# Four edits to an encoder step: decayed rows read from the accumulator, v's pieces over two steps, later background sums, a row scale from a sum of squares

## The chip, the cores and the metric

The kernel runs on one core of a Trainium2 chip. Its engines are named as the profile names them: PE is TensorE's matrix product and PEld its weight load, DVE is VectorE, ACT is ScalarE, POOL is GpSimd and SP is SyncE, which here only issues transfers. Times are microseconds on the device. The kernel before was run three times: 3076.58, 3070.44 and 3073.78 us; the median is 3073.78. One further execution was profiled, and all rows below come from it.

## What is computed

One layer of a streaming encoder, on 4096 prompt rows and 32 sample rows of width 1024. Every row is normalised, scaled and shifted (by vectors that come from a conditioning vector c), and multiplied by one wide weight w_in. The product is cut into z, x, B, C, dt, u, v and a gate g for two mixers. Both results go side by side through w_out, and the rows are normalised again and added to the input.

```
h = rms_norm(x, g_pre) * (1 + scale) + shift                 # scale, shift from silu(c) @ w_ada + b_ada
z, xbc, dt_raw, u, v, gt = split(h @ w_in)

# mixer A: 16 heads of 64 channels, state 128 long
xbc = silu(causal_conv(xbc))                                 # 4 taps; gives xs, B, C
dt  = softplus(dt_raw + dt_bias);  a = -exp(a_log)
a_cum = cumsum(dt * a)                                       # within a chunk
decay = exp(a_cum[l] - a_cum[s]) for s <= l, else 0
y_diag = ((C . B) * decay * dt) @ xs                         # within the chunk
decay_end = exp(a_cum[last] - a_cum)
chunk_states = B^T @ (decay_end * dt * xs)                   # what the chunk adds to the state
h_c = exp(a_cum[last]) * h_(c-1) + chunk_states              # carried from chunk to chunk
y = y_diag + exp(a_cum) * (C @ h_prev) + d_skip * xs
ssd_out = y * silu(z)

# mixer B: 8 groups of 128 channels, chunks of 128 rows
v_n = layer_norm(v)
gmlp_out = silu(gt) * u * (tril(w_s) @ v_n + b_s)

out = x + gate * rms_norm(concat(ssd_out, gmlp_out) @ w_out)
```

Beside the rows, the last conv inputs, the last state and the sample's v_n are returned.

## The kernel before

**Blocks and steps.** The prompt goes through in NB = 8 blocks of T = 512 rows; the sample's 32 rows ride along in block 3. Channels stand on the partitions, rows in the free direction. A block consists of nine steps k = 0 to 8 over w_in, two column groups of 256 a step (the table `SUPER`): step 0 makes B and C, step 1 the first two pairs of heads p0 and p1 (x and z of 128 channels each), steps 2 to 7 a pair p(k) and a group g(k-2) of mixer B, step 8 the groups g6 and g7. Between step 0 and step 1 lie the output projection of the block before (`out_proj`, drawn through the generator `outs`) and the product for v (`v_stage`). All wide products are made in float16 with each operand split into a high and a low part, three matrix products for one (`PARTS`): the high part is an ACT copy, the low part a subtraction on DVE or POOL (`split`, L274 and L275).

**Two forms of the product.** Blocks 0 and 1 use plain products (`plain_step`, weight tiles of 512 KB, four a step). Blocks 2 to 7 use a seven-product scheme of Strassen's kind (`super_step`, seven tiles a step, products 256 rows wide). It needs sums of weight blocks, which are made once. That is the background work of the first two blocks: in block 0 the weights are loaded, scaled and split (`stage_load`, `stage_scale`), and in block 1 `sums_load`, `sums_scale`, `sums_first` and so on load pairs of them again from DRAM, add and subtract them on DVE, split them on DVE and POOL and store the sums (L395 to L431). A sums job works in one of three areas of SBUF; the list `places` in block 1 gives each job the point at which it starts, and its area.

**What sets the order.** There are two devices. `later(n, f)` puts a function into a list that `tick()` works off: f issues its instructions n ticks later. TensorE's loops call `tick` every twelve products in a `super_step`, 14 ticks a step, and every six in a `plain_step`, 16 ticks a step; an output projection has 64 ticks, v 32. So the lag of a `later` is a place in TensorE's stream of products. Then a scheduler puts each engine's instructions in an order by the priority with which they were issued: `shifted(-150, f)` makes f more urgent, `behind` makes the sums' functions less urgent by 200. Each engine works off its own order strictly, so an instruction that waits holds up all behind it. Loads stand on SP's queue in the same way: weights (wt, wm), the rows L and E, and the sums' loads are behind one another there.

**The path of one pair of heads.** The conv (`conv`, DVE, three to four passes, then a SiLU on ACT, L805) gives xsT. `pair_rows` loads the two rows of cumulative decay as L and E (L1125 loads E), `pair_decay` and `pair_exp` make the decay from them on ACT and `pair_mask` multiplies by C.B on POOL. `pair_xt` (L1152) transposes xsT on TensorE into an accumulator bank ps_xt. `pair_xdt` multiplies it by dt on DVE, from the bank into xdt; `pair_xde` multiplies xdt by the decay to the chunk's end on POOL, into xde (both L1167, in `pair_times`). `pair_state` (L1175) makes the chunk states ps_s from xde on TensorE, `pair_carry` (L1197) carries the state from chunk to chunk on DVE into hc, and `pair_y` makes ps_y from xdt and L and ps_o from hc. `pair_sum`, `pair_gate` and `add_mix` join them. The factors dt, a_cum and the decay to the end (tile dep, array st.de) are made once a block in `dt_cumsum` (L889: a subtraction from an accumulator bank on DVE, L891: exponential on ACT).

**v.** `v_stage` makes v for the four chunks of 128 rows of a block, `v_moments` and `v_norm` their means and scales, and then each chunk's two halves are normalised on DVE into a piece vt of 128x512 (`v_split_half`, L1078) and split (ACT, POOL). Eight pieces a block, for which `v_split` is called at ticks 0, 3, 6 and 9 and its halves one tick apart. A vt lies in one of five buffers (`tmp2(prompt, ...)`), which it shares with E and with other intermediate tiles, mx and ms among them.

**Row scale.** Before the first block, gcol and scol (the scale and shift of a row, for 16 combinations of column tile and stream) are multiplied by a power of two a_sc, so that the float16 parts of h are in range. It comes from the bound max(|gcol| sqrt(1024) + |scol|), over the partitions by a transpose and a product on TensorE (L644 to L665). In the sources as in the profile, ps_... are accumulator banks (eight), hTp the normalised rows, wt and wm weights, xp the x columns of the product with their halo, zs the z columns.

## Time and profile before

| | |
|---|---|
| median of three runs | 3073.78 us |
| the profiled execution, time | 3074.91 us |
| its span | 3073.2 us |
| busy: PE, DVE, ACT, POOL | 2830.3, 1746.7, 1529.6, 1281.7 us |
| mean granted clock of TensorE | 0.972 of full speed |

The span is the time from the first to the last instruction that the profiler saw. TensorE is busy most of it. A row of the view of waits gives the idle time of an engine just ahead of a group of its instructions, by what ended it; for TensorE those are the places in which products stood still. The boundaries of the stretches, read from the timeline: block 0 about 62 to 410 us, the output projection and v of block 1 to 575, block 1's steps to 862, then blocks 2 to 7 of some 320 to 380 us each up to 2966, and the last output projection. A granted clock of 1.00 is 2.4 GHz, 0.50 is 1.2 GHz.

### The profile page before, as it was taken

What the parts mean: (1) busy time and instruction counts of PE and PEld (TensorE: products, weight loads), DVE (VectorE), ACT (ScalarE), POOL (GpSimd) and SP (SyncE); (2) the same over time, 40 slices, a digit from 0 to 9 for tenths busy, and PEclk for the clock granted to TensorE, in tenths of its full rate; (3) what the DMA queues carried; (4) which work ended last, traced back from release to release, by engine and by line L of the source; (5) the groups of instructions that cost most, each with busy time, mean ns of one, the idle gap of its engine ahead of it and who ended that gap; (6) DMA issues with size and microseconds to landing.
All of it is one profiled execution on the core that took longest, in us unless ns stands there. A gap on an engine that the chain in (4) does not pass through costs nothing.

```text
span 3073.2 us, 54218 instructions
## 1 busy us (share of the span) xinstructions
PE 2830.3 (92%) x20754; PEld 1881.3 (61%) x20754; DVE 1746.7 (57%) x3808; ACT 1529.6 (50%) x3234; POOL 1281.7 (42%) x1193
## 2 busy tenths in 40 slices
PE   7989898688999999989998999999999999999987
PEld 2434443344655887458874588747885588648863
DVE  4768686775664556355564554735455544526452
ACT  4577654567653554436544355444544354415531
POOL 2456654576632443224542245323543254204540
PEclk8999999899999999999999999999999999999999
DMA  9766468876435665265562666546663666556652
GB/s 316 237 211 199 146 203 297 267 240 212 151 104 201 200 195 177 90 205 178 179 201 75 215 201 195 176 155 211 192 214 102 222 195 188 182 173 198 197 159 57
DMA packets 269053, 577.36 MB, mean 188 GB/s; under 512 B 27898, under 2 KB 115170, under 8 KB 268792
## 3 DMA queue, kind: packets, MB, share of 16 engines
q1 hardware_dynamic: 246840, 500.86, 51.5%
q0 software_dynamic: 21952, 73.04, 6.4%
q8 instruction: 162, 2.65, 0.4%
q14 instruction: 99, 0.81, 0.1%
HBM read 499.82 MB, written 73.97 MB: 187 GB/s over the span
## 4 chain that ended last, share of the span: by engine, by line
PE 42%; DVE 12%; ACT 8%; DMA 5%; POOL 5%; issue 2%; SPq 0%; POOLq 0%; ACTq 0%; DVEq 0%
PE ps_proj L778 18%; PE ps_out L951 11%; PE ps_v L1016 5%; DMA wm<-vd 2%; DVE ms L1289 2%; DMA L<-acdp 2%; PE ps_y L1208 2%; PE ps_s L1175 1%; DVE vt L1078 1%; PE ps_out L1375 1%; POOL acc L1102 1%; POOL mix L1242 1%; PE ps_o L1212 1%; ACT L805 1%; DMA E<-acdp 1%
## 5 line engine op out<-in xcount | busy, mean ns | idle before, releaser
L778 PE MATMUL ps_proj<-hTp,wt 128*128 128x256 f16 x9072 | 1047.4, 274 | 44.6 <-ACT zs L731 26.5
L778 PEld LDWEIGHTS <-wt 128*128 128x128 f16 x9072 | 887.6, 98 | 157.2 <-issue 41.2
L951 PE MATMUL ps_out<-wm,mix 128*128 128x512 f16 x2880 | 646.2, 382 | 29.3 <-DVE dep L889 15.3
L951 PEld LDWEIGHTS <-mix 128*128 128x128 f16 x2880 | 280.9, 98 | 356.7 <-issue 28.1
L749 PE MATMUL ps_proj<-hTp,wt 128*128 128x512 f16 x1728 | 401.8, 389 | 2.5 <-DMA wt<-wd 2.5
L749 PEld LDWEIGHTS <-wt 128*128 128x128 f16 x1728 | 171.3, 100 | 203.0 <-issue 20.1
L1134 ACT ACTIVATE L<-L,acp 128x128 f32<-128x128 f32 x512 | 166.8, 391 | 165.6 <-DMA L<-acdp 150.5
L1016 PE MATMUL ps_v<-wm,hTp 128*128 128x512 f16 x1008 | 222.6, 381 | 17.8 <-DMA wm<-vd 17.8
L1224 POOL TENSOR_TENSOR mix<-mix,E 128x512 f32<-128x512 f32 x64 | 95.5, 1492 | 308.4 <-DVE E L1220 308.4
L1145 POOL TENSOR_TENSOR L<-L,cb 128x512 f32<-128x512 f32 (+1 forms) x144 | 168.1, 1180 | 104.7 <-ACT L L1139 103.0
L729 DVE SCALAR_TENSOR_TENSOR xp<-ps_proj,scw,xp 128x256 f32<-128x256 f32 x132 | 62.4, 480 | 233.5 <-PE ps_proj L778 221.5
L1016 PEld LDWEIGHTS <-hTp 128*128 128x128 f16 x1008 | 98.7, 98 | 139.2 <-issue 22.1
L818 DVE SCALAR_TENSOR_TENSOR xsT<-xp,cols,xsT 128x512 f32<-128x512 f32 (+1 forms) x216 | 182.8, 849 | 1.7
L275 POOL TENSOR_TENSOR mix<-ms,mix 128x512 f16<-128x512 f32 x64 | 90.8, 1421 | 220.6 <-ACT mix L274 220.6
L1102 POOL TENSOR_TENSOR acc<-acc,sq 128x512 f32<-128x512 f32 (+1 forms) x126 | 148.3, 1178 | 43.9 <-ACT sq L1098 42.4
L275 POOL TENSOR_TENSOR v<-vt,v 128x512 f16<-128x512 f32 (+1 forms) x66 | 83.7, 1297 | 174.9 <-ACT v L274 174.8
L275 POOL TENSOR_TENSOR hTp<-ta,hTp 128x512 f16<-128x512 f32 x60 | 71.3, 1189 | 202.7 <-ACT hTp L274 202.6
L810 ACT ACTIVATE halo_p<-xp 128x3 f32<-128x3 f32 x96 | 19.5, 203 | 220.5 <-DVE xp L729 219.9
L1167 POOL TENSOR_TENSOR xde<-xdt,dep 128x512 f32<-128x512 f32 x64 | 70.8, 1107 | 138.1 <-DVE xdt L1167 129.2
L274 ACT ACTIVATE mix<-ms 128x512 f16<-128x512 f32 x128 | 79.5, 627 | 83.4 <-DVE ms L1289 82.7
L1175 PE MATMUL ps_s<-xde,bt 128*128 128x128 f32 (+1 forms) x528 | 79.5, 296 | 41.2 <-POOL xde L1167 41.2
L1098 ACT ACTIVATE sq<-mix 128x512 f32<-128x512 f32 x120 | 74.8, 626 | 78.4 <-POOL mix L1242 59.0
(428 smaller groups left out, 4703.9 us busy)
## 6 DMA issues: line engine op xcount, KB each, us to landing
wt<-wd SPq DMA_DIRECT2D x414, 512.0 KB, 4.1
wm<-od SPq DMA_DIRECT2D x104, 512.0 KB, 3.5
wm<-vd SPq DMA_DIRECT2D x92, 512.0 KB, 4.9
L<-acdp SPq DMA_DIRECT2D x128, 256.0 KB, 4.1
sums<-in_w_in_dram SPq DMA_DIRECT2D x38, 512.0 KB, 6.5
wd<-wt POOLq DMA_DIRECT2D x36, 512.0 KB, 4.8
stg<-in_w_in_dram SPq DMA_DIRECT2D x64, 256.0 KB, 5.2
E<-acdp SPq DMA_DIRECT2D x128, 128.0 KB, 4.4
```

The costliest lines, as they stand in the source:

```text
L274: nc.scalar.activation(hi, src, AF.Copy)
L275: eng.tensor_tensor(lo, src, hi, op=ALU.subtract)
L749: nc.tensor.matmul(ps[pi].rearrange("p (h t) -> p h t", h=2), wt[:, pi, a, q * P:(q + 1) * P], prompt.h[:, 2 * kh:2 * kh + 2, b, q, :], st ...
L778: nc.tensor.matmul(ps, wt[:, pi, a, q * P:(q + 1) * P], prompt.h[:, slot, b, q, :], start=(starts and h == 0 and n == 0), stop=(n == 11), ...
L818: nc.vector.scalar_tensor_tensor(dst, xp[:, k:k + Ts], w(k), dst, op0=ALU.mult, op1=ALU.add)
L951: nc.tensor.matmul(ps[c], x(kk, a, c), w[:, kk, b, :], start=(first and n == 0), stop=(last and n == 5))
L1016: nc.tensor.matmul(ps, prompt.h[:, slot, a, q, i * P:(i + 1) * P], wt[q // 2][:, q % 2, b, :], start=(starts and n == 0), stop=(n == 11), ...
L1102: eng.tensor_tensor(st.accb if last else st.acc, st.acc, sq, op=ALU.add)
L1134: nc.scalar.activation(L[:, c, :], L[:, c, :], AF.Relu, scale=-1.0, bias=st.ac[:, c, 2 * j + hh:2 * j + hh + 1])
L1145: nc.gpsimd.tensor_tensor(w.L[hh], w.L[hh], st.cb[j // 4][0:st.Q], op=ALU.mult)
L1175: nc.tensor.matmul(ps_s[:, c * P:(c + 1) * P], st.bt[j // 4][0:st.Q, c, :], w.xde[:, c, :], start=True, stop=True)
L1224: nc.gpsimd.tensor_tensor(w.m, w.m, w.E, op=ALU.add)
```

## The change

Four places are changed.

1. `dt_cumsum` multiplies st.de by dt on DVE, behind the exponential. `pair_xdt` then makes both xde and xdt on DVE, each straight from the accumulator bank, xde first; `pair_xde` on POOL is gone.
2. The eight pieces of v come one every four ticks, first halves of the four chunks at ticks 0, 4, 8 and 12, second halves at 16 to 28, over two steps instead of one; the split follows two ticks later instead of one. (`v_split` is gone. The sample's pieces come at ticks 0 and 4.)
3. Sums jobs start at ticks 40 + 16n and 48 + 16n instead of 18 + 18n and 27 + 18n of block 1. The third area's places are as before.
4. The row scale comes from the sum of squares of gcol sqrt(2048) and scol sqrt(2), with two ACT instructions, one product on TensorE (`ssq_total`) and the helper that other scales use (`pow2_of_ssq`).

```diff
-    bnd = const.tile([P, 2, KT], F32, name="bnd")
...
-    nc.vector.tensor_scalar(bnd, gcol, math.sqrt(DM), None, op0=ALU.mult)
...
-    nc.vector.tensor_reduce(bmx, bnd, axis=AX.XY, op=ALU.max)
-    ps = psum("ps_bmx")
-    nc.tensor.transpose(ps[0:1, 0:P], bmx, ident)
...
-    nc.vector.tensor_scalar(a_inv.bitcast(I32), e_i, B23, -12.0 * B23, op0=ALU.mult, op1=ALU.add)
+    sq2 = const.tile([P, 2], F32, name="sq2")
+    sqj = const.tile([P, 2, 2 * KT], F32, name="sqj")
+    for i, (t, f) in enumerate(((gcol, math.sqrt(2 * DM)), (scol, math.sqrt(2.0)))):
+        nc.scalar.activation(sqj[:, i], t.rearrange("p s k -> p (s k)"), AF.Square, scale=f, accum_out=sq2[:, i:i + 1])
+    nc.vector.tensor_tensor(sq2[:, 0:1], sq2[:, 0:1], sq2[:, 1:2], op=ALU.add)
+    pow2_of_ssq(ssq_total(sq2[:, 0:1]), [P, 1], "wp", a_sc, a_inv)
...
         nc.scalar.activation(st.de, st.de, AF.Exp)
+        nc.vector.tensor_tensor(st.de, st.de, st.dt, op=ALU.mult)
+        st.dd = st.de
         later(9, dt_rows, st)
...
         for c in range(n):
-            later(3 * c, v_split, st, c, mv, r)
+            sp = st.v[c].bitcast(F16).rearrange("p (h a d) -> p h a d", h=2, a=2)
+            st.vsplit.append(sp)
+            for half in range(2):
+                later((4 if st is prompt else 1) * (c + 4 * half), v_split_half, st, c, half, sp, mv, r)
...
-    def v_split(st, c, mv, r):
-        Q = st.Q
-        sp = st.v[c].bitcast(F16).rearrange("p (h a d) -> p h a d", h=2, a=2)
-        for half in range(2):
-            later(half, v_split_half, st, c, half, sp, mv, r)
-        st.vsplit.append(sp)
...
-        later(1, split, sp[0:Q, half, 0], sp[0:Q, half, 1], t, nc.gpsimd)
+        later(2, split, sp[0:Q, half, 0], sp[0:Q, half, 1], t, nc.gpsimd)
...
     def pair_xdt(st, j, w, ps):
         Q, n, nm = st.Q, st.nch, st.name
-        w.xdt = wk.tile([P, n, P], F32, tag="xdt" + nm, name="xdt", bufs=1)[0:Q]
-        pair_times(st, j, nc.vector, w.xdt, ps[0:Q, 0:n * P].rearrange("q (c m) -> q c m", c=n), st.dt)
-        later(1, shifted, -150, pair_xde, st, j, w)
-
-    def pair_xde(st, j, w):
-        w.xde = wk.tile([P, st.nch, P], F32, tag="xde" + st.name, name="xde", bufs=1)[0:st.Q]
-        pair_times(st, j, nc.gpsimd, w.xde, w.xdt, st.de)
+        w.xdt, w.xde = [wk.tile([P, n, P], F32, tag=t + nm, name=t, bufs=1)[0:Q] for t in ("xdt", "xde")]
+        src = ps[0:Q, 0:n * P].rearrange("q (c m) -> q c m", c=n)
+        pair_times(st, j, nc.vector, w.xde, src, st.dd)
+        pair_times(st, j, nc.vector, w.xdt, src, st.dt)
...
-            places = [(18 + 18 * n, f[:, 0:3072]) for n in range(10)]
-            places += [(27 + 18 * n, f[:, 3072:6144]) for n in range(9)]
+            places = [(40 + 16 * n, f[:, 0:3072]) for n in range(10)]
+            places += [(48 + 16 * n, f[:, 3072:6144]) for n in range(9)]
             places += [(114 + 30 * n, spare(prompt.h)) for n in range(3)]
```

TensorE's own order is the same in both kernels but for ten places where neighbours change. The order of DVE moves at three kinds of place. The first is DVE behind v of block 4, at about 1754 us of the trace: vt are v's pieces, xp and zs the columns of the product, the last row the conv of pair p0. Before:

```order
L1078 TENSOR_SCALAR vt<-v,mvp,nrp 128x512 x8
L729 SCALAR_TENSOR_TENSOR xp<-ps_proj,scw,xp 128x256 x2
L729 SCALAR_TENSOR_TENSOR zs<-ps_proj,scw,zs 128x256 x2
L729 SCALAR_TENSOR_TENSOR xp<-ps_proj,scw,xp 128x256
L815 TENSOR_SCALAR xsT<-xp,cols 128x512
L818 SCALAR_TENSOR_TENSOR xsT<-xp,cols,xsT 128x512
```

In the changed kernel (its lines are numbered some 13 to 18 lower) the same place reads:

```order
L1063 TENSOR_SCALAR vt<-v,mvp,nrp 128x512 x5
L716 SCALAR_TENSOR_TENSOR xp<-ps_proj,scw,xp 128x256
L1063 TENSOR_SCALAR vt<-v,mvp,nrp 128x512
L716 SCALAR_TENSOR_TENSOR xp<-ps_proj,scw,xp 128x256
L716 SCALAR_TENSOR_TENSOR zs<-ps_proj,scw,zs 128x256 x2
L716 SCALAR_TENSOR_TENSOR xp<-ps_proj,scw,xp 128x256
L802 TENSOR_SCALAR xsT<-xp,cols 128x512
L805 SCALAR_TENSOR_TENSOR xsT<-xp,cols,xsT 128x512
```

Five of the eight pieces still stand together ahead of the first xp, the sixth behind it, and the last two no longer stand ahead of the conv.

The second place is DVE in block 1's steps, between the first pair's carry (hc, Hp) and the second pair's xdt; sums and hTp stand here for the two areas in which the sums' jobs work. Before:

```order
L424 TENSOR_TENSOR sums<-sums 128x512
L1197 SCALAR_TENSOR_TENSOR hc<-hc,dcp,ps_s 128x64 x6
L1197 SCALAR_TENSOR_TENSOR Hp<-hc,dcp,ps_s 128x64 x2
L424 TENSOR_TENSOR hTp<-hTp 128x512
L275 TENSOR_TENSOR sums<-sums 128x512
L275 TENSOR_TENSOR hTp<-hTp 128x512
L429 TENSOR_TENSOR sums<-sums 128x512
L429 TENSOR_TENSOR hTp<-hTp 128x512
L1167 TENSOR_TENSOR xdt<-ps_xt,dtp 128x512
```

And in the changed kernel:

```order
L1179 SCALAR_TENSOR_TENSOR hc<-hc,dcp,ps_s 128x64 x6
L1179 SCALAR_TENSOR_TENSOR Hp<-hc,dcp,ps_s 128x64 x2
L1149 TENSOR_TENSOR xde<-ps_xt,dep 128x512
L424 TENSOR_TENSOR sums<-sums 128x512
L412 TENSOR_SCALAR sums<-sums,sw 128x1024
L424 TENSOR_TENSOR hTp<-hTp 128x512
L417 TENSOR_TENSOR sums<-sums 128x512
L275 TENSOR_TENSOR sums<-sums 128x512
L429 TENSOR_TENSOR sums<-sums 128x512
L418 TENSOR_TENSOR sums<-sums 128x512
L1149 TENSOR_TENSOR xdt<-ps_xt,dtp 128x512
```

The second pair's xde stands right behind the carry, ahead of the sums' passes, and its xdt behind seven of them.

The third place is DVE in block 4 at the third pair, one step after the first place: mx and mix are outputs of the mixers. Before:

```order
L1259 SCALAR_TENSOR_TENSOR mx<-ps_sp,gvc,sp 128x512
L1197 SCALAR_TENSOR_TENSOR hc<-hc,dcp,ps_s 128x64 x6
L1197 SCALAR_TENSOR_TENSOR Hp<-hc,dcp,ps_s 128x64 x2
L1167 TENSOR_TENSOR xdt<-ps_xt,dtp 128x512
L1219 SCALAR_TENSOR_TENSOR mix<-xsT,cols,ps_y 128x512
```

And in the changed kernel:

```order
L1241 SCALAR_TENSOR_TENSOR mx<-ps_sp,gvc,sp 128x512
L1063 TENSOR_SCALAR vt<-v,mvp,nrp 128x512
L1179 SCALAR_TENSOR_TENSOR hc<-hc,dcp,ps_s 128x64 x2
L1149 TENSOR_TENSOR xde<-ps_xt,dep 128x512
L1179 SCALAR_TENSOR_TENSOR hc<-hc,dcp,ps_s 128x64 x4
L1179 SCALAR_TENSOR_TENSOR Hp<-hc,dcp,ps_s 128x64 x2
L1063 TENSOR_SCALAR vt<-v,mvp,nrp 128x512
L1149 TENSOR_TENSOR xdt<-ps_xt,dtp 128x512
L1201 SCALAR_TENSOR_TENSOR mix<-xsT,cols,ps_y 128x512
```

The two late pieces stand here, one on either side of a carry, and the next pair's xde has moved into that carry.

## Rows read from the trace of the kernel before

**Rows 1.** Page, part 1: busy us (share of the span) and instructions per engine.
```profile
PE 2830.3 (92%) x20754; PEld 1881.3 (61%) x20754; DVE 1746.7 (57%) x3808; ACT 1529.6 (50%) x3234; POOL 1281.7 (42%) x1193
```

**Rows 2.** TensorE's waits: waiting line <- releaser: total us, times, longest.
```profile
PE ps_s L1175 <- POOL xde L1167: 41.2, 11, 6.6
PE ps_xt L1152 <- ACT xsT L805: 38.1, 7, 22.6
PE ps_proj L778 <- ACT zs L731: 26.5, 21, 1.7
...
PE ps_out L951 <- DVE dep L889: 15.3, 4, 12.7
...
PE ps_proj L778 <- DVE xp L729: 7.1, 5, 1.4
```

**Rows 3.** The same view in 62:410 us, then in 575:862 us.
```profile
PE ps_s L1175 <- POOL xde L1167: 14.1, 6, 5.4
...
PE ps_s L1175 <- POOL xde L1167: 27.1, 5, 6.6
```

**Rows 4.** Windows: length; busy PE, PEld, DVE, ACT, POOL; clock, DMA share, GB/s.
```profile
575.00:862.00 287.00, 233.66 (x1421) 132.72 (x1420) 206.24 (x371) 186.29 (x329) 177.16 (x166) 0.91 0.62 198
...
696.00:700.00 4.00, 3.32 (x12) 2.42 (x13) 0.00 (x0) 3.96 (x6) 2.00 (x3) 0.50 1.07 371
```

**Rows 5.** Instructions of two lines: ns shortest/median/longest, first and last start.
```profile
L1167 DVE TENSOR_TENSOR xdt<-ps_xt,dtp x64: 678/692/693, 181.0 to 2940.2; 128x512 f32<-128x512 f32 x64
L1167 POOL TENSOR_TENSOR xde<-xdt,dep x64: 1037/1049/1492, 183.2 to 2943.2; 128x512 f32<-128x512 f32 x64
...
L1078 DVE TENSOR_SCALAR vt<-v,mvp,nrp x64: 529/1366/5212, 153.0 to 2781.6; 128x512 f32<-128x512 f32 x64
```

**Rows 6.** Timeline: start, length, instruction, in brackets idle before and releaser.
```profile
221.88 0.68 DVE L1167 TENSOR_TENSOR xdt<-ps_xt,dtp 128x512 f32<-128x512 f32 x1
...
227.35 1.05 POOL L1167 TENSOR_TENSOR xde<-xdt,dep 128x512 f32<-128x512 f32 x1
...
228.45 2.08 PE L1175 MATMUL ps_s<-xde,bt 128*128 128x128 f32 x8 [5.38 <-POOL xde L1167]
...
729.59 1.04 POOL L1167 TENSOR_TENSOR xde<-xdt,dep 128x512 f32<-128x512 f32 x1 [0.58 <-DVE xdt L1167]
...
730.68 2.07 PE L1175 MATMUL ps_s<-xde,bt 128*128 128x128 f32 x8 [6.58 <-POOL xde L1167]
```

**Rows 7.** Timeline of block 4 behind v; last, SP queue's wait.
```profile
1753.93 7.94 DVE L1078 TENSOR_SCALAR vt<-v,mvp,nrp 128x512 f32<-128x512 f32 x8
...
1762.32 5.40 PE L778 MATMUL ps_proj<-hTp,wt 128*128 128x256 f16 x48 [1.42 <-DVE xp L729]
...
1769.03 2.79 PE L778 MATMUL ps_proj<-hTp,wt 128*128 128x256 f16 x24 [1.31 <-DMA wt<-wd]
...
1774.07 0.66 PE L1152 MATMUL ps_xt<-ident,xsT 128*128 128x128 f32 x4 [2.25 <-ACT xsT L805]
...
SPq L1125 <- POOL v L275: 45.6, 11, 17.3
```

**Rows 8.** Timeline of DVE in block 1: two passes of a sums job.
```profile
561.36 0.75 DVE L412 TENSOR_SCALAR sums<-sums,sw 128x1024 f32<-128x1024 f32 x1
...
562.14 0.69 DVE L417 TENSOR_TENSOR sums<-sums 128x512 f32<-128x512 f32 x1
```

**Rows 9.** Timeline of block 1: output projection, dep's exponential, first transposes.
```profile
471.70 7.54 PE L951 MATMUL ps_out<-wm,mix 128*128 128x512 f16 x24 [12.66 <-DVE dep L889]
...
472.15 0.25 ACT L891 ACTIVATE dep<-dep 128x64 f32<-128x64 f32 x1
...
612.68 1.11 PE L1152 MATMUL ps_xt<-ident,xsT 128*128 128x128 f32 x4 [22.63 <-ACT xsT L805]
```

**Rows 10.** Timeline of the prologue: the row scale's first and last steps.
```profile
47.10 0.17 DVE L640 SCALAR_TENSOR_TENSOR gcol<-gcol,cols 128x16 f32<-128x16 f32 x1
...
56.20 0.23 DVE L664 TENSOR_SCALAR gcol<-gcol,a_sc 128x16 f32<-128x16 f32 x1
```

More of the change, by code (lines that the diff above doesn't have):

```diff
@@ L642, in hybrid_step_kernel @@
                                    op0=ALU.add, op1=ALU.mult)
-    bnd = const.tile([P, 2, KT], F32, name="bnd")
-    bnd2 = const.tile([P, 2, KT], F32, name="bnd2")
-    nc.vector.tensor_scalar(bnd, gcol, math.sqrt(DM), None, op0=ALU.mult)
-    nc.vector.tensor_single_scalar(bnd.bitcast(I32), bnd.bitcast(I32), 0x7FFFFFFF, op=ALU.bitwise_and)
-    nc.vector.tensor_single_scalar(bnd2.bitcast(I32), scol.bitcast(I32), 0x7FFFFFFF, op=ALU.bitwise_and)
-    nc.vector.tensor_tensor(bnd, bnd, bnd2, op=ALU.add)
-    bmx = const.tile([P, 1], F32, name="bmx")
-    nc.vector.tensor_reduce(bmx, bnd, axis=AX.XY, op=ALU.max)
-    ps = psum("ps_bmx")
-    nc.tensor.transpose(ps[0:1, 0:P], bmx, ident)
-    bm1 = const.tile([1, 1], F32, name="bm1")
-    nc.vector.tensor_reduce(bm1, ps[0:1, 0:P], axis=AX.X, op=ALU.max)
-    nc.vector.tensor_scalar_max(bm1, bm1, 2.0 ** -40)
-    ps = psum("ps_bm1")
-    nc.tensor.matmul(ps[:, 0:1], ones[0:1, :], bm1, start=True, stop=True)
-    e_i = const.tile([P, 1], I32, name="e_i")
-    nc.vector.tensor_copy(e_i.bitcast(F32), ps[:, 0:1])
-    nc.vector.tensor_single_scalar(e_i, e_i, 23, op=ALU.logical_shift_right)
-    nc.vector.tensor_scalar(a_sc.bitcast(I32), e_i, -B23, (127.0 + 12 + 127) * B23, op0=ALU.mult, op1=ALU.add)
-    nc.vector.tensor_scalar(a_inv.bitcast(I32), e_i, B23, -12.0 * B23, op0=ALU.mult, op1=ALU.add)
+    sq2 = const.tile([P, 2], F32, name="sq2")
[4 more added lines that the diff above has]
+    pow2_of_ssq(ssq_total(sq2[:, 0:1]), [P, 1], "wp", a_sc, a_inv)
     nc.vector.tensor_scalar(gcol, gcol, a_sc, None, op0=ALU.mult)
```

## The prediction

> **What bounds the kernel now.** I read the page first: TensorE is busy in 2830.3 of 3073.2 us [rows 1], so it stands still for 243 us, and every other engine is far from full. So what a change is worth is read from TensorE's own waits, not from the busy time that it moves. The table of waits [rows 2] comes next. The reader is to see that its two longest entries touch the edits: TensorE's state product (ps_s) waits 41.2 us for xde, which GpSimd (POOL) makes, and its transposes (ps_xt) wait 38.1 us for xsT, the conv result, of which one single wait is 22.6 us. The third entry, 26.5 us in 21 pieces for the copies of ScalarE (ACT), hangs on table loads and loads of L in the middle of the blocks; nothing in the diff is on that path, and it stays. Restricted to stretches, the xde waits turn out to be all in block 0 (14.1 us in 6) and block 1 (27.1 us in 5) [rows 3]: 14.1 + 27.1 = 41.2. These are the two blocks in which GpSimd and VectorE (DVE) also split weights. Block 1's steps are the worst stretch of the kernel: TensorE 233.7 of 287 us, at a granted clock of 0.91 [rows 4].
>
> **xde on DVE.** Removed: 64 GpSimd instructions of 1.05 us (up to 1.49) and the hop from xdt to xde. Added: 64 DVE instructions like xdt, 0.692 us each, 44 us of DVE busy time, 8 smaller ones of the sample, and one 128x64 multiplication per block. xdt's spread is the argument for the price: 678 to 693 ns in all 64, while the xde of GpSimd goes from 1037 to 1492 and the vt of DVE from 529 to 5212 [rows 5]. It reads the accumulator, and nothing that GpSimd did in the meantime touched it.
>
> The Trainium skill (GPSIMD Engine Reference, section 8, Key points) says that GpSimd shares its SBUF interfaces with VectorE and that the two contend when a DVE instruction is in a 2-port mode or has two SBUF inputs. A product whose one large input is the accumulator is neither, and the constant xdt agrees; by the rule vt is the other case, and its spread agrees as well. If xde on DVE were stretched as vt's median is, 1366 against 529, the 64 would take 114 us instead of 44, which is 18 more in the 16 of blocks 0 and 1 and would eat a third of the sum below; by the row it stays at 44.
>
> What the hop is worth: TensorE's waits end with xde. Two cases [rows 6]. In block 0, xdt is over at 222.56, but xde starts only at 227.35 behind other GpSimd work and TensorE has waited 5.38 us when it comes: with xde in xdt's place the wait is gone altogether. In block 1, xde starts at 729.59, as soon as xdt is done, and TensorE has waited 6.58 us: here the hop is only the last 1.1 us, DVE itself was late. So the ends are 11 x 1.04 = 11.4 us and 41.2 us. I take 30: all but 1 us of block 0, and 17 of block 1, since in the new order the second xde of block 1 stands ahead of the sums' operations that xdt stood behind (second place shown in the order). After such a wait TensorE also runs at half clock: 0.50 granted in 696 to 700, 1.2 of 2.4 GHz [rows 4], so 2 us of those 4 are lost; five waits of 27.1 / 5 = 5.4 us in block 1 make up to 10 us, and I take 5.
>
> The added DVE time is hidden in blocks 2 to 7, where TensorE's order is the same and xde is wanted many us after xdt. In blocks 0 and 1 it costs between 0 and 16 x 0.692 = 11 us; I take 4. The multiplication of de by dt is put at nothing: it waits for ACT's exponential, which was over 0.70 us after the subtraction freed TensorE (471.70 to 472.40) [rows 9]; what is queued behind it on DVE in that place are splits for the output projection, and even all 8 blocks at 1 us are 8.
>
> **v's pieces.** Before, all eight vt stand together on DVE, 7.94 us in block 4, and behind them the xp copy that TensorE needs: it waits 1.42 us for that, then 1.31 us for weights, then 2.25 us for xsT [rows 7]. The loads of E take the same five buffers as vt, wait 45.6 us in the kernel for the pieces' splits on GpSimd, and stand on SP's queue ahead of the weight loads [rows 7]; that is the second way by which the burst comes to TensorE. In the new order five pieces stand ahead of the first xp copy, one behind it, and two are a step later. Three of eight, 3 us, is more than the 1.42, and two fewer pieces of 1 us each ahead of it let E go some 2 us earlier. Over the kernel the waits for xp are 7.1 us and those for xsT without the 22.6 are 15.5 [rows 2]: the ends are 0 and 22.6, and I take 16. What is late next is the two pieces in the following step, 1.4 us each, between two xde and the carries; if a buffer is not free there, the carry waits and with it ps_o.
>
> The 22.6 us in block 1 [rows 9] have the same form (ACT's splits of v ahead of the copy of xp, then DVE's pieces ahead of the conv), but there the sums' operations fill the gaps, and seven of the eight pieces still precede the conv. Ends 0 and 22.6; I take 6, nearer to the block-4 rows.
>
> **Sums.** Loads fall at ticks 40 to 184 instead of 18 to 180. Eleven of the 22 jobs fell before tick 112, where block 1's first weights are through and its steps begin; now nine do. So two jobs more come into the worst stretch. A job is one pass of 0.75 us and six of about 0.69 us on DVE [rows 8], some 4.9 us: 0 to 9.8 us, and I take 5 as a loss. In return the start of the output projection is free of them, but the 12.66 us that TensorE stands there is for dep, the subtraction that frees a bank [rows 9], and in the new order nearly as many passes of the sums stand ahead of it as before. Ends 0 and 12.66 gained; I take 0. SP's loads of the sums move behind some of the loads of w_out, which are then a little earlier; at nothing, since TensorE's waits for wm there are small.
>
> **Row scale.** From gcol to the scaled gcol it is 47.10 to 56.20, 9.1 us [rows 10], with two TensorE hops in it. Now it is two short ACT squares, one hop, and seven instead of ten weight passes in between. Ends 0 and 9.1; I take 3.
>
> **Sum.** 30 + 5 - 4 + 16 + 6 - 5 + 3 = 51 us, against the profiled execution of 3074.9 us (span 3073.2), which is 1.1 above the median of 3073.8. 3074.9 - 51 = 3024; on the median's footing 3023, and I say 3025.
>
> **Rivals.**
> - *DVE becomes the bound in blocks 0 and 1.* For it: DVE is busy in 206.2 of 287 us there [rows 4] and gets 9.8 + 5.5 more; the wait for GpSimd becomes one for DVE. Against it: xde has priority in the order. Then xde gives its low end and the clock nothing: 11.4 - 11 + 16 - 9.8 + 3 = 10, with some of the low costs not at their worst 20: 3055. Chance 0.22.
> - *More goes than I count.* The 22.6 us and the 12.66 us are both queues on DVE that get shorter; if two thirds of each go, 15 - 6 + 8 = 17 more, and all of xde's 41.2 another 11: 2997. Chance 0.14.
> - *Slower: the sums' areas.* An area is loaded again after 16 ticks instead of 18. If the earlier job's last DVE pass is not over by then, SP stands on that load, and the weight loads behind it are late. Thirteen jobs are in the steps; it decides when each costs TensorE over 51 / 13 = 3.9 us. At 5 us: 65 - 51 = 14 slower, 3089. Against it: in the profile TensorE hardly waits for weights in block 1. Chance 0.06.
> - *It does not spread.* Six of eight pieces still stand together, and if the two late ones cost a carry wait in each block (16 + 6 lost) and DVE's load the rest, nothing is left: 3074. Chance 0.06.
>
> **Numbers.** Forecast 3025 with 0.52. A measurement of this kernel can tell about 0.2%, 6 us, from no change. Faster by more than that are the forecast and the first two rivals, 0.88; within it the last, 0.06; slower the third, 0.06. The range runs from just below the second rival to beyond the first, 2992 to 3062; the forecast's own range, from terms at half their distance to the ends, is 3005 to 3045.
>
> **What would show it.** In the changed kernel ps_s should wait for DVE's xde under 12 us in all; GpSimd be about 70 us less busy and DVE about 45 more, with xde at 0.69 us; the waits of ps_proj for xp after v gone and those of ps_xt for xsT under 1 us a block from block 2 on; the granted clock of block 1's steps above 0.93. I am wrong if block 1's steps last as long as before (xde not on its path), if ps_o's waits for the carry appear after v, or if weights from SP are waited for in block 1.

## The result and the profile after

The kernel before took 3072.11 us (median of 4 runs, 3066.95 to 3076.58), the changed kernel 3039.90 us (median of 4, 3035.94 to 3042.92). The medians lie 32 us apart; the ratio on record is 0.9886, 95% interval 0.9873 to 0.9899, which is 35 us of 3072 (31 to 39). Forecast was 3025, 49 us less than 3074. The direction and the range were right; some 14 us of the gain did not come, and one term, that of xde, was twice too large, as the following shows. The profiled execution of the changed kernel took 3035.94 us, so it lies 4 us below its median.

Part 1 of the page, which answers to [rows 1]:

```profile
PE 2822.3 (93%) x20751; PEld 1878.1 (62%) x20752; DVE 1781.1 (59%) x3884; ACT 1525.0 (50%) x3236; POOL 1200.8 (40%) x1121
```

POOL is 80.9 us less busy and DVE 34.4 us more. TensorE stands still for 211.7 us instead of 242.9. TensorE's waits in the changed kernel (waiting line, releaser, total us, times, longest), to be laid beside [rows 2]:

```profile
PE ps_proj L765 <- ACT zs L718: 25.9, 21, 2.1
PE ps_xt L1137 <- ACT xsT L792: 19.9, 8, 15.2
PE ps_s L1157 <- DVE xde L1149: 17.6, 5, 6.8
PE ps_out L940 <- DVE dep L876: 16.7, 4, 14.2
...
PE ps_y L1190 <- issue: 5.5, 1, 5.5
...
PE ps_o L1194 <- DVE hc L1179: 4.7, 1, 4.7
PE ps_o L1194 <- ACT zs L744: 4.0, 1, 4.0
```

The waits for xp (7.1 us in five) have gone from the list, those for xsT without the longest have fallen from 15.5 to 4.7, and the waits for xde from 41.2 to 17.6. In their place stand waits that were short or absent: ps_y, ps_o for hc and for zs. The xde waits by stretch, 59.5 to 404 us (block 0) and then 566.5 to 853 us (block 1's steps), beside [rows 3]:

```profile
PE ps_s L1157 <- DVE xde L1149: 3.1, 2, 1.7
...
PE ps_s L1157 <- DVE xde L1149: 14.5, 3, 6.8
```

In block 0 they went from 14.1 to 3.1 us, in block 1 from 27.1 to 14.5, and there the releaser is DVE now. In the windows view the steps of block 1 (566.5 to 853 us) take 286.5 us at a granted clock of 0.92, against 287.0 at 0.91 in [rows 4]. But the two stretches do not hold the same work: 1461 products now, 1421 before. A fair pair is block 1 from its cumulative-sum products to those of block 2, with 2058 products in both (length; busy PE, PEld, DVE, ACT, POOL; granted clock, DMA share, GB/s), before and after:

```profile
450.18:893.40 443.22, 369.88 (x2058) 195.92 (x2057) 309.12 (x552) 262.60 (x461) 248.12 (x252) 0.93 0.67 221
```

```profile
442.87:882.96 440.09, 373.55 (x2058) 196.71 (x2057) 319.04 (x560) 260.23 (x460) 238.55 (x243) 0.92 0.67 225
```

So block 1 is 3.1 us shorter: TensorE stands still for 66.5 instead of 73.3 us, and its products take 3.7 us longer. That block 1's steps would last as long as before was a condition under which the prediction called itself wrong, and it all but came.

The instructions of the two lines (ns shortest/median/longest), beside [rows 5]:

```profile
L1149 DVE TENSOR_TENSOR xde<-ps_xt,dep x64: 672/691/693, 177.9 to 2900.5; 128x512 f32<-128x512 f32 x64
...
L1063 DVE TENSOR_SCALAR vt<-v,mvp,nrp x64: 528/546/2749, 150.6 to 2781.8; 128x512 f32<-128x512 f32 x64
```

The price of xde was right: 0.691 us in the middle of all 64, against 0.692. vt's median fell from 1366 to 546 ns, but this says little: 34 of the 64 pieces took over 0.6 us before and 29 do now, so the middle piece only changed sides. All 64 together take 59.2 us instead of 67.4.

**Where the time went.** TensorE's order is nearly the same in both kernels, so one of its instructions can serve as a mark. The small products of the cumulative sum stand once in each block. Their starts for blocks 0, 1 and 2 (timeline), before and then after:

```profile
98.38 0.33 PE L882 MATMUL ps_ac<-dtt,tri 128*128 128x64 f32 x2
...
450.18 0.33 PE L882 MATMUL ps_ac<-dtt,tri 128*128 128x64 f32 x2
...
893.40 0.33 PE L882 MATMUL ps_ac<-dtt,tri 128*128 128x64 f32 x2
```

```profile
95.66 0.33 PE L869 MATMUL ps_ac<-dtt,tri 128*128 128x64 f32 x2
...
442.87 0.33 PE L869 MATMUL ps_ac<-dtt,tri 128*128 128x64 f32 x2
...
882.96 0.33 PE L869 MATMUL ps_ac<-dtt,tri 128*128 128x64 f32 x2
```

The first mark is 2.7 us earlier (prologue). From mark to mark block 0 takes 347.2 instead of 351.8, and block 1 440.1 instead of 443.2. From the third mark to the last transposes of block 7 (2939.46 and 2899.87) it is 2016.9 instead of 2046.1, so 29.2 of 39.6 us come from blocks 2 to 7, for which the prediction had 16. Of these, 20.8 us are time in which TensorE stood still (99.2 before, 78.4 now). The other 8.4 are busy time, and that differs from execution to execution for the same products: 1935 to 1951 us in the traces of this case.

Behind v of block 4, which [rows 7] showed before, the changed kernel's timeline reads (start, length, idle before in brackets):

```profile
1735.48 2.67 DVE L1063 TENSOR_SCALAR vt<-v,mvp,nrp 128x512 f32<-128x512 f32 x2 [1.05 <-POOL v L275]
1738.07 0.47 DVE L716 SCALAR_TENSOR_TENSOR xp<-ps_proj,scw,xp 128x256 f32<-128x256 f32 x1
```

```profile
1739.78 8.02 PE L765 MATMUL ps_proj<-hTp,wt 128*128 128x256 f16 x72
1748.34 0.66 PE L1137 MATMUL ps_xt<-ident,xsT 128*128 128x128 f32 x4 [0.54 <-ACT xsT L792]
```

DVE still waits for one of the five buffers, but xp is no longer behind all eight pieces, and of TensorE's 1.42 + 1.31 + 2.25 us only 0.54 are left.

**Block 1.** Where the 12.6 us that left the xde waits there went can be seen on DVE:

```profile
639.10 0.68 DVE L1149 TENSOR_TENSOR xde<-ps_xt,dep 128x512 f32<-128x512 f32 x1
646.07 0.69 DVE L424 TENSOR_TENSOR sums<-sums 128x512 f32<-128x512 f32 x1 [6.29 <-POOL sums L275]
646.68 3.08 DVE L412 TENSOR_SCALAR sums<-sums,sw 128x1024 f32<-128x1024 f32 x1
649.67 2.47 DVE L424 TENSOR_TENSOR hTp<-hTp 128x512 f32<-128x512 f32 x1
...
654.59 0.68 DVE L1149 TENSOR_TENSOR xdt<-ps_xt,dtp 128x512 f32<-128x512 f32 x1
...
683.15 1.63 DVE L424 TENSOR_TENSOR sums<-sums 128x512 f32<-128x512 f32 x1 [6.54 <-POOL sums L275]
...
686.86 0.68 DVE L1149 TENSOR_TENSOR xde<-ps_xt,dep 128x512 f32<-128x512 f32 x1
```

```profile
655.38 2.06 PE L1190 MATMUL ps_y<-L,xdt 128*64 128x128 f32 x16 [5.45 <-issue]
...
687.60 2.08 PE L1157 MATMUL ps_s<-xde,bt 128*128 128x128 f32 x8 [5.59 <-DVE xde L1149]
```

This is the second place that was shown of the order; in the trace its pair is the third of the block, not the second, as the text there and the prediction have it. xde stands ahead of the sums' passes as the order promised, and TensorE does not wait for it (4.58 us before). But its xdt stands behind seven of them. The first waits 6.29 us for a split on POOL, and two more take 3.08 and 2.47 us where [rows 8] have 0.75 and 0.69. TensorE then waits 5.45 us at ps_y, which reads xdt (its record names no releaser; xdt ends at 655.27, 0.1 us before it). At the next pair both stand behind such a pass, and TensorE waits 5.59 us for xde (6.53 before). So the wait is no longer for POOL's xde, but for DVE standing at a sums pass.

DVE stood at these passes before the change too, only for another engine. Its two waits at them in block 1's steps, before (575 to 862 us) and after (566.5 to 853):

```profile
DVE sums L275 <- ACT sums L274: 17.3, 6, 6.9
...
DVE sums L424 <- POOL sums L275: 6.9, 3, 3.5
```

```profile
DVE sums L424 <- POOL sums L275: 18.6, 6, 6.5
...
DVE sums L275 <- ACT sums L274: 4.1, 5, 1.8
```

Together they were 24.2 us and are 22.7.

### The profile page after: what moved, and what is told of

Read it like the earlier page. It is cut to its first block, busy times and chain, and to the rows that moved or that the text cites. A ratio compares the mean times of both kernels' runs of the same rounds, so it can differ in the third digit from the quotient of the medians.

```text
span 3034.0 us, 54221 instructions
## 1 busy us (share of the span) xinstructions
PE 2822.3 (93%) x20751; PEld 1878.1 (62%) x20752; DVE 1781.1 (59%) x3884; ACT 1525.0 (50%) x3236; POOL 1200.8 (40%) x1121
## 3 DMA queue, kind: packets, MB, share of 16 engines
q8 instruction: 163, 2.67, 0.4%
## 4 chain that ended last, share of the span: by engine, by line
PE 41%; DVE 10%; ACT 8%; DMA 6%; POOL 5%; issue 4%; SPq 0%; POOLq 0%; ACTq 0%; DVEq 0%
PE ps_proj L765 18%; PE ps_out L940 11%; PE ps_v L1005 4%; DMA L<-acdp 2%; DVE ms L1271 2%; DMA wm<-vd 2%; PE ps_y L1190 2%; PE ps_s L1157 1%; PE ps_out L1357 1%; POOL mix L1224 1%; POOL mix L1213 1%; ACT L792 1%; POOL acc L1087 1%; ACT L L1119 1%; PE ps_o L1194 1%
## 5 line engine op out<-in xcount | busy, mean ns | idle before, releaser
L1206 POOL TENSOR_TENSOR mix<-mix,E 128x512 f32<-128x512 f32 x64 | 95.7, 1496 | 358.7 <-DVE E L1202 292.0
L274 ACT ACTIVATE mix<-ms 128x512 f16<-128x512 f32 x128 | 79.3, 627 | 80.9 <-DVE ms L1271 79.7
L1271 DVE TENSOR_TENSOR ms<-mix,sb 128x512 f32<-128x512 f32 x128 | 101.2, 805 | 17.3 <-POOL hTp L275 9.2
L1213 POOL TENSOR_TENSOR mix<-mix,us 128x512 f32<-128x512 f32 x64 | 81.8, 1282 | 59.9 <-ACT us L718 42.7
```

The costliest lines, as they stand in the source:

```text
L1206: nc.gpsimd.tensor_tensor(w.m, w.m, w.E, op=ALU.add)
L1213: nc.gpsimd.tensor_tensor(m, m, w.d[1], op=ALU.mult)
L1271: nc.vector.tensor_tensor(t, m, sb, op=ALU.mult)
```

## The experiments

Each run is timed beside the kernel before on the same chip, 4 to 11 executions of each run. Lengths by the marks above, from one profiled execution each (us): prologue to the first mark, block 0, block 1, and blocks 2 to 7 to the last transposes.

| kernel | ratio to before, 95% interval | first mark | block 0 | block 1 | blocks 2-7 |
|---|---|---|---|---|---|
| before | 1 | 98.4 | 351.8 | 443.2 | 2046.1 |
| changed | 0.9886 (0.9873 to 0.9899) | 95.7 | 347.2 | 440.1 | 2016.9 |
| e1 xde on DVE alone | 0.9952 (0.9939 to 0.9966) | 96.7 | 346.9 | 441.5 | 2043.4 |
| e2 v's pieces alone | 0.9932 (0.9919 to 0.9946) | 95.1 | 353.4 | 441.1 | 2027.6 |
| e3 later sums alone | 1.0022 (1.0012 to 1.0031) | 98.5 | 354.6 | 447.3 | 2049.4 |
| e4 row scale alone | 0.9984 (0.9975 to 0.9994) | 95.9 | 352.2 | 443.4 | 2049.0 |
| e5 changed, no sums arithmetic | 0.9684 (0.9665 to 0.9703) | 95.8 | 345.7 | 382.7 | 2023.6 |
| e6 changed, all splits on POOL | 0.9927 (0.9909 to 0.9945) | 94.1 | 346.1 | 455.1 | 2025.1 |
| e7 changed, second pass later | 0.9882 (0.9862 to 0.9901) | 95.9 | 344.8 | 440.9 | 2015.2 |
| e8 changed, bank read by ACT | 0.9879 (0.9862 to 0.9896) | 95.4 | 345.3 | 439.4 | 2023.4 |
| e9 changed, first splits on DVE | 0.9869 (0.9853 to 0.9885) | 95.4 | 346.4 | 439.1 | 2023.7 |
| e10 changed, old sums places | 0.9867 (0.9850 to 0.9883) | 95.5 | 346.5 | 440.3 | 2020.6 |
| e11 e9 and e10 together | 0.9861 (0.9846 to 0.9875) | 95.9 | 346.8 | 438.4 | 2022.4 |
| e12 e5 with xde on POOL | 0.9766 (0.9748 to 0.9784) | 95.5 | 352.5 | 395.0 | 2030.4 |

Kernels that differ in nothing a stretch contains still differ there by about 3 us in block 0 and 10 in blocks 2 to 7. A single first mark, 95.1 in e2, is 3 us early without an edit that touches it. For block 1, which nearly all runs change, the scatter is not known; a difference of 2 or 3 us there is taken for none.

**e1 to e4: each edit alone on the kernel before.** Their edits are the four numbered parts of the change, one each; of every part only the line that tells most is shown:

```diff
# e1
-    later(1, shifted, -150, pair_xde, st, j, w)
+    pair_times(st, j, nc.vector, w.xde, src, st.dd)
# e2
-    later(3 * c, v_split, st, c, mv, r)
+    later((4 if st is prompt else 1) * (c + 4 * half), v_split_half, st, c, half, sp, mv, r)
# e3
-    places = [(18 + 18 * n, f[:, 0:3072]) for n in range(10)]
+    places = [(40 + 16 * n, f[:, 0:3072]) for n in range(10)]
# e4
-    nc.vector.tensor_reduce(bmx, bnd, axis=AX.XY, op=ALU.max)
+    pow2_of_ssq(ssq_total(sq2[:, 0:1]), [P, 1], "wp", a_sc, a_inv)
```

> The kernel before with the first edit alone (de times dt, xde and xdt both on DVE from the accumulator). Theory A, the prediction's own sum: the edit is worth 30 + 5 - 4 = 31 us, so about 3041 against 3072, and nearly all of it lies in blocks 0 and 1. Theory B, from the two traces set side by side at TensorE's transposes: blocks 0 and 1 together gained only 7 to 8 us between them with all four edits, since DVE itself is late there behind passes of the sums and splits; so this edit alone gives 0 to 8 us, 3064 to 3072, and TensorE's waits for xde become waits for xdt, hc or other DVE results.

> The kernel before with v's pieces over two steps alone. Theory A (the prediction): 16 us in blocks 2 to 7 and 6 in block 1, so 22 us, about 3050. Theory B (the traces side by side: each of blocks 2 to 7 was 3 to 7 us shorter, 29 us in all, and nearly all of it between v and the first transposes): about 29 us, 3043, and none of it in block 1.

> The kernel before with the later sums jobs alone. Theory A (the prediction): 5 us slower, 3077. Theory B: the first xsT wait of block 1 shrank from 22.6 to 15.2 us, and if it was the sums passes ahead of the conv that went, this edit alone gives that, some 7 us, 3065. If the wait belongs to v's pieces, nothing: 3072.

> The kernel before with the row scale from a sum of squares alone. Both theories: 3 us from the prologue, 3069, which is near what five rounds can tell; in the trace the scaled gcol should come some 3 us earlier and all that follows be earlier by the same.

Measured, of 3078: e1 0.48%, 14.8 us faster (10 to 19); e2 0.68%, 20.9 us faster; e3 0.22%, 6.8 us slower; e4 0.16%, 4.9 us faster. They sum to 33.8 us, beside 35 for the whole: the edits add up, as far as intervals of 3 to 4 us either way on each can tell. e1's time lies between the theories, half of what A said and more than B allowed; by the marks its blocks 0 and 1 are 6.6 us shorter, as B said, and the rest stands in no one stretch. For e2 the prediction's 22 was nearer than B's 29. e3 went A's way in its size, not B's: the first xsT wait of block 1 did shrink, to 19.2 us, but the waits for xde there grew to 33.9.

e2's gain came although its waits for POOL's xde grew, from 41.2 to 57.2 us in all. They are here for 62 to 410 and then for 410 to 862 us; before they were 14.1 and 27.1:

```profile
PE ps_s L1171 <- POOL xde L1163: 22.4, 5, 7.4
...
PE ps_s L1171 <- POOL xde L1163: 31.0, 5, 7.2
```

In e1 the waits of block 0 for xde fell to 1.8 us, as forecast, but others came (93 to 403.5 us of e1):

```profile
PE ps_ssq L300 <- DVE ssb L298: 6.5, 2, 3.3
PE ps_xT L238 <- DVE ntp L209: 5.2, 1, 5.2
PE ps_xt L1154 <- ACT xsT L805: 2.9, 2, 2.6
PE ps_o L1211 <- ACT zs L757: 2.1, 1, 2.1
PE ps_s L1174 <- DVE xde L1166: 1.8, 2, 1.4
```

Before, the first two and zs stood there (62 to 410 us) with 2.6, 3.7 and 0.4 us. Of 12.3 us gained at ps_s some 7 came back at these three, and block 0 is 4.9 us shorter.

**e5: is block 1 the sums?**

```diff
     def sums_scale(w):
-        nc.scalar.activation(w.a, w.a, AF.Identity, scale=w.s[0])
-        nc.vector.tensor_scalar(w.b, w.b, w.s[1], None, op0=ALU.mult)
-        later(1, behind, sums_first, w)
+        nc.scalar.activation(w.o.bitcast(F16), w.a, AF.Identity, scale=w.s[0])
+        for i, s in enumerate(SUMS):
+            later(2 + 2 * i, behind, sums_store, w, s)
...
```

> The changed kernel without the arithmetic of the 22 sums jobs: the loads stay, and in place of the passes on ACT, DVE and POOL there is one ACT copy a job and the four stores (so the products of blocks 2 to 7 are not the reference's). Theory C: TensorE's waits of block 1 (14.2 for dep, 15.2 for xsT, 14.5 + 5.5 + 4.7 + 2.1 for xde, xdt and hc) are all DVE standing at, or working on, passes of the sums; then at least 35 of these 56 us go, ratio to before about 0.977. Rival D: DVE is late there for its own pair work and v, and the sums fill gaps; then under 15 us go, ratio above 0.984.

Measured 0.9684: about 62 us less than the changed kernel, and block 1 57.4 us shorter, with nothing else in the table moved beyond its scatter. So block 1 is the sums, and D falls. The waits for dep, xsT and xde of 14.2, 15.2 and 14.5 us are now (384 to 800 us):

```profile
PE ps_xt L1140 <- ACT xsT L795: 11.0, 1, 11.0
PE ps_out L943 <- DVE dep L879: 3.8, 1, 3.8
PE ps_s L1160 <- DVE xde L1152: 2.8, 1, 2.8
```

Block 1 from mark to mark, beside the line above:

```profile
441.49:824.23 382.74, 359.25 (x2058) 191.58 (x2057) 183.13 (x409) 208.97 (x371) 174.75 (x197) 0.98 0.76 255
```

Of the 57.4 us, 43.0 are time in which TensorE stood still, and 14.3 come from the products themselves, made at a granted clock of 0.98 instead of 0.92. Theory C is borne out in size, but not in its wording: 11.0 of the 15.2 us for xsT are still there, and the run takes the passes off ACT and POOL as well as off DVE, so it does not tell which engine's part held the block up.

**e6, e7 and e9: which part of the sums?** One edit each on the changed kernel:

```diff
# e6
-        split(o[:, 0:512], o[:, 512:1024], src, nc.vector if s in (2, 5) else nc.gpsimd)
+        split(o[:, 0:512], o[:, 512:1024], src, nc.gpsimd)
# e7 (and the places at 40 + 18n, 49 + 18n)
-        later(4, behind, sums_second, w, a11, a21)
+        later(7, behind, sums_second, w, a11, a21)
# e9
-        split(o[:, 0:512], o[:, 512:1024], src, nc.vector if s in (2, 5) else nc.gpsimd)
+        split(o[:, 0:512], o[:, 512:1024], src, nc.vector if s in (1, 2) else nc.gpsimd)
```

> The changed kernel with all four splits of a sums job on POOL instead of two on DVE and two on POOL: 44 DVE passes of 0.69 us (30 us) fewer, 44 POOL passes of some 1.2 us (53 us) more, and POOL's stores no longer wait for DVE (20.5 us in block 1's steps). Theory C1, DVE's busy time is what is late: TensorE's waits in block 1 fall by 10 us or more, ratio to before 0.985 or less (the changed kernel has 0.9886). Theory C2, DVE is late because its in-order passes stand and wait for POOL's splits (18.6 us in 6 in block 1's steps): more splits on POOL make that wait longer, no gain or a loss, 0.989 or more, with DVE's waits for POOL's sums above 18.6.

> The changed kernel with the second pass of a sums job 7 ticks behind the first instead of 4 and the jobs of an area 18 ticks apart instead of 16 (from 40 and 49). By theory C2 the pass that waits for POOL's split (18.6 us in 6) is issued when the split is done, the passes of xde behind it come sooner, and 8 to 15 us go: ratio 0.984 to 0.986. By C1 the same passes are there and only later: 0.9886 within 0.002.

> The changed kernel with the first two splits of a sums job on DVE and the last two on POOL (the changed kernel has the last of each pair on DVE). The number of passes on either engine is the same; what goes is that DVE's second and third pass of a job wait for a split on POOL. Theory C2 (the waits between the two engines make DVE late): DVE's waits of L424 for POOL's sums, 18.6 us in block 1's steps, go, and 8 to 15 us of the time with them, ratio to before 0.984 to 0.986. Theory C1 (the busy time of the passes makes it late): nothing changes, 0.9886 within 0.002.

e6 is some 12.6 us slower than the changed kernel and its block 1 15 us longer. C1 as it was stated falls. But the run takes less off DVE than was expected: the 110 passes that are left of 154 take 120.1 us instead of 140.5, and DVE's whole busy time falls by 11 us (1781.1 to 1770.0), while POOL's grows by 47 (1200.8 to 1248.0). That DVE's busy time has a part in it is not excluded. DVE's waits in e6's block 1 steps (569 to 863 us):

```profile
DVE sums L424 <- POOL sums L275: 18.9, 7, 6.5
...
DVE sums L429 <- POOL sums L275: 9.2, 4, 3.8
```

That is 28.1 us for POOL instead of 18.6, as C2 said. But e7 and e9 go against C2 as it was stated. In e9's steps (567.8 to 855 us) the wait of L424 for POOL is gone, and the first waits of DVE read:

```profile
DVE sums L275 <- ACT sums L274: 10.6, 5, 4.3
DVE ntp L209 <- ACT junk L204: 10.3, 2, 7.8
```

The first of these was 4.1 us in the changed kernel. TensorE still waits 15.3 us for xde and 18.6 for xsT, and block 1 takes 439.1 us. The ratio 0.9869 cannot be told from 0.9886. So with one wait taken out of the chain of a sums job (ACT, DVE, POOL and back) others showed, and the block stayed as long. What sets the length of that chain in block 1 stays open.

**e8: the bank that dep holds.**

```diff
-        nc.vector.tensor_copy(st.ac.rearrange("q c h -> q (c h)"), ps[0:Q, 0:n * NH])
+        nc.scalar.activation(st.ac.rearrange("q c h -> q (c h)"), ps[0:Q, 0:n * NH], AF.Copy)
...
-        nc.vector.tensor_tensor(st.de, ps[0:Q, 256:256 + n * NH].rearrange("q (c h) -> q c h", h=NH),
-                                st.ac, op=ALU.subtract)
+        nc.scalar.activation(st.de.rearrange("q c h -> q (c h)"), ps[0:Q, 256:256 + n * NH], AF.Copy)
+        nc.vector.tensor_tensor(st.de, st.de, st.ac, op=ALU.subtract)
```

> The changed kernel with the two reads of ps_ac's bank in dt_cumsum by ACT copies, and dep's subtraction from SBUF behind them on DVE. The wait of 14.2 us in block 1's output projection is for the bank that DVE's subtraction frees. If ACT comes at once, 10 to 14 us go and the ratio is 0.984 to 0.985; if ACT is as late as DVE (it has the sums' scaling and splits too), or if the next products then wait for DVE's wm copies, it is 0.9886 within 0.002. The prediction had put this wait's change at nothing with ends 0 and 12.66.

0.9879, the second case: ACT is nearly as late as DVE. The wait fell from 14.17 to 10.42 us, and the next one on TensorE's path grew from 15.20 to 20.94:

```profile
458.20 2.29 PE L940 MATMUL ps_out<-wm,mix 128*128 128x512 f16 x5 [10.42 <-ACT dep L876]
...
600.46 1.12 PE L1137 MATMUL ps_xt<-ident,xsT 128*128 128x128 f32 x4 [20.94 <-ACT xsT L792]
```

**e10 and e11: the changed kernel with the old places, and with e9's splits beside.** e10 is the changed kernel without e3's edit; e11 adds e9's.

> The changed kernel with the sums jobs at their old places (18 + 18n, 27 + 18n), so the other three edits together. The later places alone cost 6.8 us on the kernel before (ratio 1.0022). If the edits add up, this is 7 us faster than the changed kernel, 0.9864; if the later places only cost while xde came over POOL, or pay beside the others, it is 0.9886 or more.

> Both of the other runs of this call together: old places of the sums jobs, the first two splits on DVE. If both theories hold, 15 to 22 us faster than the changed kernel, ratio 0.982 to 0.984. If only the places count 0.9864, if neither 0.9886.

0.9867 and 0.9861. By the ratios they are 6 and 8 us below the changed kernel, and e11's interval (to 0.9875) just touches the changed kernel's (from 0.9873). e11 beats the kernel before; whether it beats the changed one these rounds do not settle, since the two did not run beside each other. Whether e3's loss is still there beside the other edits stays open: by the ratio e10 stands where it would if the edits add up (0.9864), but its interval overlaps the changed kernel's, and by the marks block 1 is the same in all of them, 438 to 440 us, where e3 alone has 447.3.

**e12: what xde is worth without the sums.** e5's edit, with the hunk of e1 undone.

> The changed kernel without the sums' arithmetic (as before: loads, one ACT copy a job and four stores remain, so the products of blocks 2 to 7 are not the reference's) and with xde back on POOL behind xdt. Beside the earlier run without the sums (ratio 0.9684; between TensorE's cumulative-sum products block 0 took 345.7 us and block 1 382.7) it is what the xde edit is worth where no sums passes stand on DVE. Theory S, the sums set block 1's length and hide what xde gains there: without them POOL's hop is on the path, block 1 takes 388 to 395 us, block 0 351 to 354, and the ratio is 0.972 to 0.974. Theory R, xde has slack in block 1 once DVE is free, and the edit is worth nothing there in either case: block 1 within 3 us of 382.7, block 0 351 to 354, ratio 0.970 to 0.971.

0.9766 against e5's 0.9684: without the sums the xde edit is worth 0.8%, 25 us. Block 0 is 6.8 us shorter by it, block 1 12.3 and blocks 2 to 7 6.8. Theory S holds (block 1 and block 0 fall where it said; its ratio was 0.974 at most, the measured 0.9766 is beyond it). With the sums' arithmetic in place the like pair is e2 and e10, between which lie the xde edit and the row scale: 6.9, 0.8 and 7.0 us in the same three stretches. So by the marks it is in block 1 alone that the sums hide the gain, 11.5 us of it. With xde on POOL and no sums, TensorE's waits in 384 to 810 us show POOL's xde again, 13.9 us where e5 has 2.8:

```profile
PE ps_s L1161 <- POOL xde L1153: 13.9, 4, 5.9
```

## Why the prediction was right in its range and wrong in one term

- **xde on DVE: 30 + 5 - 4 = 31 forecast, 15 measured (e1), and about 15 beside v's pieces (e2 to e10 20 us by the ratios, less e4's 4.9).** This term makes up the whole of the gain that did not come. The step that failed is "17 of block 1, since in the new order the second xde of block 1 stands ahead of the sums' operations that xdt stood behind (second place shown in the order)". That was read rightly for one pair and taken for all. At that pair TensorE's wait went from 4.58 us to nothing; at the next two it was 6.53 and 6.58 and is 5.59 and 6.77, since their xde stands behind sums passes on DVE. With the sums' passes in place block 1 is 1.7 us shorter by the edit alone (443.2, e1 441.5) and 0.8 beside v's pieces (e2, e10). With the sums' arithmetic gone the same edit gives 12.3 there (e12, e5). The gain was there, and the background work hid it. The 5 us for the clock went with it: over the same products of block 1, 0.92 was granted instead of 0.93. Where the edit did gain, without the sums, TensorE's products took 4.0 us less (363.22 to 359.25 in block 1, at 0.98 instead of 0.97).
- **Block 0: 13 of the 30 forecast, 5 to 7 measured.** The waits for xde did go (14.1 to 1.8 in e1), and waits of TensorE for other late DVE and ACT results took over about 7 us. The prediction named no "late next" there.
- **Blocks 2 to 7: nothing forecast for xde.** Alone it gives 2.7 us there (e1), beside v's new places 7.0 (e2 to e10), without the sums 6.8 (e12 to e5): within the scatter of 10, but of one sign. e2's trace names 3.8 us of it: TensorE waits four times for POOL's xde, where it never did before. That v's late splits on POOL are the reason is argued.
- **v's pieces: 16 + 6 = 22 forecast, 21 measured (e2).** In blocks 2 to 7 it is 18.5 by the marks, against 16, and 13.9 of that is time in which TensorE stood still. In block 1 it is 2.1 against 6; the 22.6 us wait was 20.2 us in e2. That the sums' passes fill the gap, which the prediction had weighed, fits but was not tried. The waits for xp are gone and SP's wait for POOL's splits of v is down from 45.6 to 33.5 us in e2, so both ways named were at work. The two late pieces cost no carry wait in blocks 2 to 7. What the prediction did not see is that xde would wait longer for POOL beside them, 57.2 us instead of 41.2.
- **Sums: 5 slower forecast, 6.8 measured alone (e3).** The price of a job was too low: 4.9 us from two short passes, where the 154 passes of the 22 jobs took 137.1 us before, 6.2 a job. Whether the loss is there beside the other edits stays open (e10).
- **Row scale: 3 forecast, 4.9 measured, 1.8 to 7.7 by its interval (e4).** The trace settles it better than the time. From gcol to the scaled gcol it was 9.1 us [rows 10], and it is 5.7 in e4 (46.20 to 51.86) and in the changed kernel (46.25 to 51.91): 3.4 us. In e1 and e2, without the edit, it is 9.1 as before. The first mark is no measure of it: in e2 it is 3.3 us early because gcol itself comes 2.6 us earlier.
- **dep's wait was put at nothing,** and it stayed (12.66 to 14.17). The reason given, nearly as many sums passes ahead of it as before, fits. The new multiplication of st.de was put at nothing as well, since ACT's exponential was over 0.70 us after the subtraction. In block 1 DVE now stands 4.9 us at it (468.92) for that exponential, but no wait of TensorE names it.
- **The signs named.** POOL fell by 81 us (70 named), DVE rose by 34 (45; the pieces vt take 8 us less in all), xde is 0.69 us and the waits for xp are gone: met. The waits for xsT from block 2 on are 4.2 us in five; one of them, 1.6 us in block 2, is over the 1 us named. Waits for xde under 12 us (17.6) and a clock above 0.93 in block 1's steps (0.92): not met. Of the other two signs of being wrong, the carry hc was waited for once in block 1, 4.7 us (2.5 in two before), and weights in block 1 for 3.2 and 2.7 us (2.5 in all before): both small.
- **The rivals.** "DVE becomes the bound" was half right: the wait for POOL did become one for DVE in block 1. How much of that is DVE's busy time, as that rival had it, and how much DVE standing at sums passes is not shown. The measured 3040 lies between the forecast and that rival's 3055.

## What to carry to other kernels

A long wait on the bounding engine is a gain only if nothing else would end at the same place. In this block ACT, DVE and POOL wait for each other in turn through the background work, and three edits that each took one wait away or made it shorter (xde, e8, e9) made the block at most 2 us shorter, with other waits in the place of the one. So first time the stretch with the background work left out (57 us here), and then what the edit gives with and without it (1 to 2 us and 12). A new order that is shown for one place holds for that place; the others have to be looked up. A mark that stands once in each block in TensorE's own order tells in one table which stretch a change touched, where totals of waits do not.

## What was not expected of the hardware

The length of DVE's passes from SBUF doubled at times when POOL worked. In the changed kernel's block 1 one and the same pass took 1.52 us at 589.42, with POOL's splits of v beside it, and 0.69 us at 615.99:

```profile
589.42 1.52 DVE L417 TENSOR_TENSOR sums<-sums 128x512 f32<-128x512 f32 x1
...
615.99 0.69 DVE L417 TENSOR_TENSOR sums<-sums 128x512 f32<-128x512 f32 x1
```

```profile
586.36 5.59 POOL L275 TENSOR_TENSOR v<-vt,v 128x512 f16<-128x512 f32 x4 [0.18 <-ACT v L274]
```

Every long pass had POOL beside it. In the changed kernel 88 passes of the sums add or subtract a 128x512 tile, both inputs in SBUF: 19 of them took over 0.8 us, and POOL worked during two thirds or more of each; the 23 with no POOL work beside them took at most 0.693. The 29 vt over 0.6 us had POOL beside them as well, and no vt without POOL took over 0.547. But POOL beside a pass does not always lengthen it: 39 of the 88 had POOL working for more than half of their length and stayed short. The 64 xde from the accumulator kept to 672 to 693 ns all the while, 47 of them with POOL working for more than half of theirs. The Trainium skill (GPSIMD Engine Reference, section 8, Key points) says that the two engines contend for shared SBUF interfaces when a DVE instruction has two SBUF inputs or is in a 2-port mode; these rows agree with it. Spreading v's pieces changed little in this: 29 of 64 are long instead of 34 (29 in e2 too, by that edit alone), 8.2 us of DVE time in all. The row at 1735.48 above is the long kind, two pieces in 2.67 us. What the long passes cost TensorE was not tried by itself.
